# Turning values, keys and K with VectorE blocks and small transfers instead of TensorE transposes, in a hybrid retention/HGRN2 decoder layer

## The chip, the cores and the metric

The kernel runs on one core of one Trainium2 chip. The metric is device time in microseconds of one execution; lower is better. Before the change, three runs took 2565.3, 2567.76 and 2568.72 us.

## What is computed

One inference step of a decoder layer with model width 2048 for two groups of tokens that share the weights: a prompt of 256 tokens with 16 learned meta tokens ahead of it, and 8 single new tokens ("samples"), each with recurrent states of its own. All 280 tokens go through the dense products together. Per layer:

```
x <- LN1(alpha*x + 0.5*SwiGLU_1(x))
x <- LN2(alpha*x + Mixer(x))
x <- LN3(alpha*x + 0.5*SwiGLU_2(x))
```

The change lies in the mixer. One projection `x @ w_in` (2048 to 20480) gives ten parts. Retention has 8 heads of width 256, HGRN2 has 16 heads of width 128. In the reference a chunk of retention is:

```
inner = einsum('bhid,bhjd->bhij', q, k) * D
o = einsum('bhij,bhjv->bhiv', inner, v) + einsum('bhid,bhdv->bhiv', q_dec, S)
S_new = exp(lg * C) * S + einsum('bhjd,bhjv->bhdv', k_dec, v)
```

HGRN2 has the same form, with a decay for each key channel that depends on the data. The results are the tokens' outputs and the new states of both branches, for the prompt and for each sample.

Two of these products sum over tokens j: the state product (`k_dec` with `v`) and the output (`inner` with `v`). The matrix unit sums over partitions, so their operands must have tokens on the partitions, while the projection leaves channels on the partitions and tokens along the rows. Values and keys therefore have to be turned, 128x128 at a time.

## The kernel before

Every dense product is done in three matmuls per 128x128 weight block, in a reduced-precision fp32 format: each operand is split into a high and a low part, and high-high, low-high and high-low are summed (`dense`, line 204). Weights stream in units of eight blocks, 512 KB (`stream`, line 170): SP issues the DMA into one of three `raw` buffers, ScalarE casts the high part `whi` (line 188), VectorE subtracts for the low part `wlo` (line 189), each with three buffers, and TensorE's matmuls (line 218) follow.

The mixer runs over eight units `u`, one retention head and two HGRN2 heads each. For each, `project` runs the groups f, q_h, i_h, q_r, k_r, v_r and then the four gate groups of the unit before. A group has two output banks; one dense step is one k of its sixteen, six matmuls. After a group, `evacuate` (line 648) takes its two banks out of PSUM. The head's own small work is done by two Python generators, `mix_hg` (line 746) and `mix_ret` (line 1085), started after i_h and v_r. `pump` (line 617), called after each dense step, counts down each generator's wait; `yield n` means that it goes on n dense steps later. The order on TensorE is thus the order of the program, written by hand with these numbers. On the other engines and on SP's queue a scheduler orders by priority, with the weight stream ahead.

What the change touches, in this order within a unit:

- `evacuate` for i_h (lines 663 to 670) and v_r (682 to 686): ScalarE copies the two banks into the tile `v`, which both share (one buffer).
- `mix_hg`: GpSimd copies the first and last 16 tokens into `ends` (750, 751). TensorE transposes four 128x128 blocks of `v` (875) and the ends (878), ScalarE copies the result to `vth` (879). Later, `turned(h)` (976) transposes the decayed keys `K`, four blocks (982), ScalarE copies them to `kth` (983). Tiny GpSimd copies (769, 773) hold back the loads of the samples' states and values until a given point. The state product follows (1022 to 1030), and the samples' state updates (998, 999).
- `mix_ret`: GpSimd copies the last 24 tokens of k and v into `tails` (1103). For each half of the head TensorE transposes two blocks of v (1107) and two of k (1114), with the tails once (1116). ScalarE copies v to `vtr` (1108); `split` makes the high and low parts `vs` (1110); k is scaled by the decay and split into `ks` straight from PSUM (1129, 1130). Then come scores (1141), state product (1168), the samples' state update on ScalarE and VectorE (1192, 1198), its read on TensorE (1211), and outputs (1226). The samples' states, `ks` and `vs` share four buffers, `smr`.

Of the kernel before, what the change touches and what calls it, by code (L numbers as in the profile page):

```python
# [18 lines left out]
P = 128  # L19
# [109 lines left out]
def trunk(ctx: ExitStack, tc: tile.TileContext, A, O):  # L129
# [417 lines left out]
    with tc.tile_pool(name="yp", bufs=1) as yp:  # L547
# [7 lines left out]
        with tc.tile_pool(name="mp", bufs=1) as mp:  # L555
# [73 lines left out]
            def project(groups):  # L629
                for grp in groups:  # L630

                    bank = mx_bank if grp[0] == (QKV_ORDER[2], 0) else acc_bank
                    outs = [bank(f"pj_{n}{c}") for n, c in grp]
                    x0s = [NMETA if n in LIVE else 0 for n, _ in grp]
                    if grp[0] == (QKV_ORDER[0], 0):
                        outs = norm1.first(block, outs, x0s)
                    elif grp[0] == (QKV_ORDER[2], 0):
                        v = st["i_h"] = tmp("v", (P, 2, T))
                        outs = norm1.second(block, outs, x0s, (v[:, 0, :], v[:, 1, :]))
                    else:  # L640
                        dense(block, KC, outs, xh, xl, [slice(x0, T) for x0 in x0s], pump)
                        outs = [(o, None) for o in outs]
                    for j in range(0, len(grp), 2):
                        w = T - x0s[j]
                        (o0, b0), (o1, b1) = outs[j : j + 2]
                        evacuate(grp[j][0], grp[j][1], grp[j + 1][1], o0[:, :w], o1[:, :w], b0, b1)

            def evacuate(n, c0, c1, o0, o1, b0, b1):
# [14 lines left out]
                elif n == "i_h":  # L663
                    v = st.pop("i_h", None)
                    if v is None:
                        v = tmp("v", (P, 2, T))
                        nc.scalar.copy(v[:, 0, :], o0)
                        nc.scalar.copy(v[:, 1, :], o1)

                    start(mix_hg(c0 // 2, st["f"], st["k"], st["q"], v), {0: 20, 2: 46}.get(c0, 4))  # L670
                elif n in ("q_r", "k_r"):
                    sc, w, x0 = (1.0, TL, NMETA) if n == "q_r" else (KSC, T, 0)
                    r = tmp(n, (P, 2, w))
                    for j, (a, b, op) in enumerate(((cos, sin, ALU.subtract), (sin, cos, ALU.add))):
                        t = tmp("rot", (P, w), bufs=2)
                        for to, o, s, x in ((r[:, j, :], o0, b0, a), (t, o1, b1, b)):
                            nc.vector.scalar_tensor_tensor(
                                out=to, in0=o, scalar=sc if s is None else s, in1=x[:, x0:],
                                op0=ALU.mult if s is None else ALU.add, op1=ALU.mult)
                        nc.vector.tensor_tensor(out=r[:, j, :], in0=r[:, j, :], in1=t, op=op)  # L680
                    st[n] = r
                elif n == "v_r":
                    v = tmp("v", (P, 2, T))
                    nc.scalar.copy(v[:, 0, :], o0)
                    nc.scalar.copy(v[:, 1, :], o1)
                    start(mix_ret(c0 // 2, st["q_r"], st["k_r"], v), 24 if c0 == 2 else 3)
# [24 lines left out]

            NB2 = LP - 2 * P
# [33 lines left out]
            def mix_hg(u, f, k, q, v):  # L746

                calm = 2
                ends = tmp("ends", (P, 2, 2, NMETA))
                nc.gpsimd.tensor_copy(ends[:, :, 0, :], v[:, :, :NMETA])  # L750
                nc.gpsimd.tensor_copy(ends[:, :, 1, :], v[:, :, T - NMETA :])
# [13 lines left out]
                def load(h):  # L765

                    sms.append(tmp("smh", (P, NS, P), bufs=2))
                    vbs.append(tmp("vbh", (P, NS, P), bufs=2))
                    nc.gpsimd.tensor_copy(sms[h][:, 0, :1], kts[0][:, 0, :1] if h else acc[:, 15:16])
                    nc.sync.dma_start(sms[h], A["sg"][2 * u + h])  # L770

                def values(h):
                    nc.gpsimd.tensor_copy(vbs[h][:, 0, :1], kts[1][:, 0, :1] if h else acc[:, 2 * P + 15 : 2 * P + 16])
                    nc.sync.dma_start(vbs[h], vrow[h].partition_broadcast(P))
# [94 lines left out]
                vt = tmp("vth", (P, 2, 2, P))  # L869
                vrow = []  # L870
                for h in range(2):

                    pt = mx_bank("pt")
                    for b in range(2):
                        nc.tensor.transpose(pt[:, b * P : (b + 1) * P], v[:, h, NMETA + b * P : NMETA + (b + 1) * P], ident)
                    x = pt[:64, 2 * P : 3 * P]
                    if h:
                        nc.tensor.transpose(x, ends.rearrange("p c a t -> p (c a t)"), ident)
                    nc.scalar.copy(vt[:, h], pt[:, : 2 * P].rearrange("p (b f) -> p b f", b=2))
                    if h:  # L880
# [93 lines left out]
                kts = []  # L974

                def turned(h):
                    kt = tmp("kth", (P, 2, P), bufs=2)
                    kts.append(kt)
                    pt = mx_bank("ptk")
                    for b in range(2):  # L980
                        t0 = NMETA + b * P
                        nc.tensor.transpose(pt[:, b * P : (b + 1) * P], K[:, h, t0 : t0 + P], ident)
                    nc.scalar.copy(kt, pt[:, : 2 * P].rearrange("p (b f) -> p b f", b=2))
# [20 lines left out]
                turned(0)  # L1004
                load(1)
                yield 4
                turned(1)
# [5 lines left out]
                if u != 1:  # L1013
                    samples(1)
                    yield 4 if u == 0 else 5

                Ss = []
                for h in range(2):
# [4 lines left out]
                    for b in range(2):  # L1023
                        nc.tensor.matmul(pst[:, (b + 1) * P : (b + 2) * P], kts[h][:, b, :], vt[:, h, b, :], start=True, stop=True)
# [9 lines left out]
                yield (8, 11, 45)[min(u, 2)]  # L1034
# [11 lines left out]
                def outputs(h):  # L1046
                    po = mx_bank("po")
                    for b in range(2):
                        o = po[:, b * P : (b + 1) * P]
                        nc.tensor.matmul(o, vt[:, h, b, :], acc[:, (2 * h + b) * P : (2 * h + b + 1) * P], start=True, stop=False)  # L1050
# [26 lines left out]
            def centre(x):  # L1077

                np_, n = x.shape[0], x.shape[1]
                m = tmp("cen", (P, n))[:np_]  # L1080
                nc.vector.tensor_reduce(out=m, in_=x, op=ALU.add, axis=mybir.AxisListType.X)
                nc.vector.tensor_scalar(out=m, in0=m, scalar1=1.0 / 256, scalar2=None, op0=ALU.mult)
                nc.vector.tensor_tensor(out=x, in0=x, in1=m.unsqueeze(2).to_broadcast([np_, n, 256]), op=ALU.subtract)

            def mix_ret(u, q, k, v):
                vt = tmp("vtr", (P, 2, 2, P))

                ks, vs = (tmp(n, (P, 2, 2, 2 * P), dt=F32R, bufs=4, tag="smr") for n in ("ks", "vs"))
# [13 lines left out]
                for i, x in enumerate((k, v)):  # L1102
                    nc.gpsimd.tensor_copy(tails[:, 2 * i : 2 * i + 2, :NB], x[:, :, 2 * P :])
                for c in range(2):
                    pt = mx_bank("pt")
                    for b in range(2):
                        nc.tensor.transpose(pt[:, b * P : (b + 1) * P], v[:, c, b * P : (b + 1) * P], ident)
                    nc.scalar.copy(vt[:, :, c, :], pt[:, : 2 * P].rearrange("p (b f) -> p b f", b=2))
                    f = slice(c * P, (c + 1) * P)
                    split(vs[:, 0, :, f], vs[:, 1, :, f], vt[:, :, c, :])  # L1110
                    yield 1
                    pt = mx_bank("pt")
                    for b in range(2):
                        nc.tensor.transpose(pt[:, b * P : (b + 1) * P], k[:, c, b * P : (b + 1) * P], ident)
                    if c == 0:
                        nc.tensor.transpose(pt[:, 2 * P : 3 * P], tails.rearrange("p i t -> p (i t)"), ident)
# [5 lines left out]
                    todo = [(pt[:, b * P : (b + 1) * P], dec[:, b, u : u + 1], [ks[:, 0, b, f]], 0, ks[:, 1, b, f]) for b in range(2)]  # L1122
# [11 lines left out]
                vts = [vt[:, 0], vt[:, 1], vs2]  # L1134
# [25 lines left out]
                yield 4  # L1160

                for c in range(2):
                    pst = mx_bank("psr")
                    f = slice(c * P, (c + 1) * P)
                    todo = [(ks[:, i, b, f], vs[:, j, b, :].rearrange("p (c f) -> p c f", c=2)) for b in range(2) for i, j in ((0, 0), (0, 1), (1, 0))]
# [13 lines left out]
                centre(vt.rearrange("p b c f -> p b (c f)"))  # L1179
# [24 lines left out]
                yield (11 if u == 0 else 15) + 2 * calm  # L1204
# [18 lines left out]
                for c in range(2):  # L1223
                    po = mx_bank("por")
                    for b, (col, l0, n, nk) in enumerate(SCORES):
                        nc.tensor.matmul(po[:, l0 : l0 + n], vts[b][:, c, :], scrs[b], start=b == 0, stop=b == 2)
# [150 lines left out]
```

## Time and profile before

| | |
|---|---|
| runs | 2565.3, 2567.76, 2568.72 us; median 2567.76 |
| profiled execution | span 2563.9 us, first to last instruction (its time outside the span isn't given) |
| TensorE clock granted | 1.000 |
| dense matmuls: ffn 1, the mixer's projections, w_out, ffn 2 | 5.3 to 745, 745.0 to 1760.5, 1760.7 to 1848.8, 1848.9 to 2547.6 us |
| DMA | 536.26 MB, mean 209 GB/s; 62.0% of the 16 engines' span on SP's queue |

The profile is one execution as the hardware profiler saw it. Its page gives busy time by engine, the span in slices, the chain of work that ended last, and the costliest groups of instructions; the trace behind it can be asked for a timeline, for waits, for DMA issues, and for busy time in chosen stretches. A group's row has the program line, engine, operation, tiles and shapes, count, busy time and mean ns of one, and behind the second bar the idle time before it with what ended that. Matmuls overlap, so a matmul's duration is longer than its share of TensorE's pace.

### The profile page before, as it was taken

Reading aid. Unit: us, or ns where it says so; the run is one execution under the profiler, and the core shown is the slowest. Engines: PE = TensorE matmul, PEld = TensorE weight load, DVE = VectorE, ACT = ScalarE, POOL = GpSimd, SP = SyncE. Lnnn points to the kernel's source line nnn. Section 1 sums busy time; section 2 is a strip of 40 time slices with the busy share of each in tenths; the row PEclk is TensorE's granted clock in tenths of the full one; section 3 lists DMA queues with packets and bytes.
Section 4 is the critical chain, followed back from the end, with each engine's and each line's share of the span. In section 5 each row is a group of like instructions: output and inputs, shape, how many; then the busy total and the mean of one; then the engine's idle time right before and its main releaser. Section 6 shows DMA issues by size and latency. Waiting matters only on the chain.

```text
span 2563.9 us, 56275 instructions
## 1 busy us (share of the span) xinstructions
PE 2553.4 (100%) x23424; PEld 2534.4 (99%) x23424; DVE 1702.8 (66%) x2827; ACT 1392.2 (54%) x2186; POOL 57.0 (2%) x152
## 2 busy tenths in 40 slices
PE   9999999999999999999999999999999999999999
PEld 9999999999999999999999999999999999999998
DVE  6444544475569878777777777777885555556555
ACT  5444444444456767767676666675564444444443
POOL 0000000000000000000000000000000000000000
PEclk9999999999999999999999999999999999999999
DMA  7555555555555876767676767675556565565554
GB/s 244 183 187 183 187 182 184 186 182 186 184 201 180 287 265 232 264 214 260 212 264 215 259 223 255 224 239 188 196 190 197 194 197 195 194 196 195 195 195 149
DMA packets 156897, 536.26 MB, mean 209 GB/s; under 512 B 17952, under 2 KB 25952, under 8 KB 156640
## 3 DMA queue, kind: packets, MB, share of 16 engines
q1 hardware_dynamic: 156352, 532.37, 62.0%
q8 instruction: 183, 3.00, 0.5%
q14 instruction: 74, 0.61, 0.1%
q10 hardware_dynamic: 288, 0.29, 0.0%
HBM read 501.99 MB, written 30.61 MB: 208 GB/s over the span
## 4 chain that ended last, share of the span: by engine, by line
PE 96%; DVE 2%; ACT 0%; issue 0%; DMA 0%; SPq 0%; ACTq 0%; DVEq 0%
PE up L218 36%; PE dn L218 19%; PE pj_i_h L218 3%; PE pj_g_r L218 3%; PE pj_q_h L218 3%; PE pj_g_h L218 3%; PE pj_a_r L218 3%; PE pj_a_h L218 3%; PE pj_f L218 3%; PE pj_q_r L218 3%; PE pj_k_r L218 3%; PE wo L218 3%; PE pj_v_r L218 3%; DVE wlo L189 1%; PE pqr L1211 1%; PE psr L1168 0%
## 5 line engine op out<-in xcount | busy, mean ns | idle before, releaser
L189 DVE TENSOR_TENSOR wlo<-raw,whi 128x1024 fp32r<-128x1024 f32 (+1 forms) x869 | 1062.2, 1223 | 740.7 <-ACT whi L188 737.3
L188 ACT CAST whi<-raw 128x1024 fp32r<-128x1024 f32 (+1 forms) x870 | 905.7, 1042 | 909.2 <-PE up L218 411.0
L218 PE MATMUL up<-xh,whi 128*128 128x280 f32 (+1 forms) x2624 | 725.6, 280 | 0.6 <-ACT whi L188 0.6
L218 PE MATMUL up<-xh,wlo 128*128 128x280 f32 (+1 forms) x2624 | 725.8, 280 | 0.4 <-DVE wlo L189 0.3
L218 PE MATMUL up<-xl,whi 128*128 128x280 f32 (+1 forms) x2624 | 725.4, 279 | 0.0
L218 PEld LDWEIGHTS up<-xh,wlo 128*128 128x128 f32 x2624 | 492.6, 189 | 1.0 <-DVE wlo L189 1.0
L218 PEld LDWEIGHTS up<-xh,whi 128*128 128x128 f32 x2624 | 492.6, 189 | 0.8 <-ACT whi L188 0.8
L218 PEld LDWEIGHTS up<-xl,whi 128*128 128x128 f32 x2624 | 492.6, 189 | 0.0
L218 PE MATMUL dn<-hh,whi 128*128 128x280 f32 (+1 forms) x1376 | 384.7, 280 | 0.0
L218 PE MATMUL dn<-hh,wlo 128*128 128x280 f32 (+1 forms) x1376 | 384.3, 279 | 0.0
L218 PE MATMUL dn<-hl,whi 128*128 128x280 f32 (+1 forms) x1376 | 384.3, 279 | 0.0
L218 PEld LDWEIGHTS dn<-hh,whi 128*128 128x128 f32 x1376 | 260.1, 189 | 0.1
L218 PEld LDWEIGHTS dn<-hl,whi 128*128 128x128 f32 x1376 | 260.1, 189 | 0.1
L218 PEld LDWEIGHTS dn<-hh,wlo 128*128 128x128 f32 x1376 | 260.1, 189 | 0.0
L218 PE MATMUL pj_k_r<-xh,whi 128*128 128x280 f32 x256 | 74.2, 290 | 0.0
L218 PE MATMUL pj_g_r<-xh,whi 128*128 128x264 f32 x256 | 74.0, 289 | 0.0
L218 PE MATMUL pj_v_r<-xh,whi 128*128 128x280 f32 x256 | 73.8, 288 | 0.0
L218 PE MATMUL pj_v_r<-xh,wlo 128*128 128x280 f32 x256 | 72.4, 283 | 0.3 <-DVE wlo L189 0.3
L218 PE MATMUL pj_g_h<-xh,whi 128*128 128x264 f32 x256 | 72.7, 284 | 0.0
L218 PE MATMUL pj_k_r<-xh,wlo 128*128 128x280 f32 x256 | 72.4, 283 | 0.0
L218 PE MATMUL pj_v_r<-xl,whi 128*128 128x280 f32 x256 | 72.3, 283 | 0.0
L218 PE MATMUL pj_k_r<-xl,whi 128*128 128x280 f32 x256 | 72.3, 283 | 0.0
(421 smaller groups left out, 5263.4 us busy)
## 6 DMA issues: line engine op xcount, KB each, us to landing
raw<-in_w_up SPq DMA_DIRECT2D x343, 512.0 KB, 4.1
raw<-in_w_in SPq DMA_DIRECT2D x320, 512.0 KB, 4.3
raw<-in_w_dn SPq DMA_DIRECT2D x172, 512.0 KB, 3.5
smr<-in_sr SPq DMA_DIRECT2D x32, 512.0 KB, 5.0
out_srs<-smr SPq DMA_DIRECT2D x32, 512.0 KB, 6.7
raw<-in_w_out SPq DMA_DIRECT2D x32, 512.0 KB, 3.9
vbr<-vrd SPq DMA_DIRECT2D x32, 256.0 KB, 4.1
smh<-in_sg SPq DMA_DIRECT2D x16, 512.0 KB, 5.2
```

What stands on the lines that cost most here:

```text
L188: nc.scalar.copy(hi[:, j:jn, :], raw[:, j:jn, :])
L189: nc.vector.tensor_tensor(out=lo[:, j0:j1, :], in0=raw[:, j0:j1, :], in1=hi[:, j0:j1, :].bitcast(F32), op=ALU.subtract)
L218: nc.tensor.matmul(o, w, t, start=start, stop=stop)
L1211: nc.tensor.matmul(pq[32 * j : 32 * j + 32, :256], qdr_at[c][:, 32 * b : 32 * b + 32], sms[2 * e + c][:, j, :], start=e + c == 0, stop=e + ...
```

## The change

All sixteen 128x128 transposes per unit on TensorE that serve v of both branches, k and K are replaced. VectorE's `transpose` turns each 32x32 block in place within its 32 partitions and 32 columns. A new function, `turned_over`, then moves the blocks to where they belong in a full transpose: 16 transfers from SBUF to SBUF, each of 32 partitions in rows of 32 values, issued on SP's queue by a generator of its own, one per dense step (`rate` 1) or two (`rate` 2).

- Values are turned at evacuation, by VectorE straight from PSUM into `v`; ScalarE copies only the ends, or the tails, and GpSimd's copies of those go. The very first i_h group goes through two spare tiles.
- k is turned right after its rotary passes, into the same single buffer `v`, and moved into the low half of `ks`, which is allocated there. The decay and split then work in place in SBUF.
- K is turned into the memory of `k` and moved into that of `f`; the tile `kth` goes.
- The split of the values and the retention state product come 6 dense steps later, the samples' update with them, and the wait ahead of the samples' read is 6 shorter. From unit 2 on, the HGRN2 state product comes 8 later and the wait behind it is 8 shorter.
- The transposes of ends, tails and the meta tokens stay on TensorE.

```diff
                 elif n == "i_h":
-                    v = st.pop("i_h", None)
-                    if v is None:
-                        v = tmp("v", (P, 2, T))
-                        nc.scalar.copy(v[:, 0, :], o0)
-                        nc.scalar.copy(v[:, 1, :], o1)
-
-                    start(mix_hg(c0 // 2, st["f"], st["k"], st["q"], v), {0: 20, 2: 46}.get(c0, 4))
+                    ends = tmp("ends", (P, 2, 2, NMETA))
+                    vt = tmp("vth", TURNED)
+                    v = tmp("v", TURNED)
+                    for j, o in enumerate(st.pop("i_h", (o0, o1))):
+                        nc.vector.transpose(v[:, j].rearrange("p b t -> p (b t)"), o[:, NMETA:LP])
+                        nc.scalar.copy(ends[:, j, 0, :], o[:, :NMETA])
+                        nc.scalar.copy(ends[:, j, 1, :], o[:, T - NMETA : T])
+                    turned_over(vt, v)
+                    start(mix_hg(c0 // 2, st["f"], st["k"], st["q"], ends, vt), {0: 20, 2: 46}.get(c0, 4))
...
+                    if n == "k_r":
+                        st["ks"] = ks = tmp("ks", (P, 2, *TURNED[1:]), dt=F32R, bufs=4, tag="smr")
+                        z = tmp("v", TURNED)
+                        nc.vector.transpose(z.rearrange("p c b t -> p c (b t)"), r[:, :, : 2 * P])
+                        turned_over(ks[:, 1].bitcast(F32), z, 2)
                     st[n] = r
                 elif n == "v_r":
-                    v = tmp("v", (P, 2, T))
-                    nc.scalar.copy(v[:, 0, :], o0)
-                    nc.scalar.copy(v[:, 1, :], o1)
-                    start(mix_ret(c0 // 2, st["q_r"], st["k_r"], v), 24 if c0 == 2 else 3)
+                    vt = tmp("vtr", TURNED)
+                    v = tmp("v", TURNED)
+                    for j, o in enumerate((o0, o1)):
+                        nc.vector.transpose(v[:, j].rearrange("p b t -> p (b t)"), o[:, : 2 * P])
+                        nc.scalar.copy(tails[:, 2 + j, : T - 2 * P], o[:, 2 * P :])
+                    turned_over(vt, v, 2)
+                    start(mix_ret(c0 // 2, st["q_r"], st["k_r"], st["ks"], vt), 24 if c0 == 2 else 3)
...
+            TURNED = (P, 2, 2, P)
...
+            def turned_over(out, z, rate=1):
+
+                def transfers():
+                    for i in range(4):
+                        for j in range(4):
+                            nc.sync.dma_start(
+                                out[32 * j : 32 * j + 32, :, :, 32 * i : 32 * i + 32],
+                                z[32 * i : 32 * i + 32, :, :, 32 * j : 32 * j + 32])
+                            if (4 * i + j + 1) % rate == 0:
+                                yield 1
+
+                start(transfers(), 1)
...
-                def turned(h):
-                    kt = tmp("kth", (P, 2, P), bufs=2)
-                    kts.append(kt)
-                    pt = mx_bank("ptk")
-                    for b in range(2):
-                        t0 = NMETA + b * P
-                        nc.tensor.transpose(pt[:, b * P : (b + 1) * P], K[:, h, t0 : t0 + P], ident)
-                    nc.scalar.copy(kt, pt[:, : 2 * P].rearrange("p (b f) -> p b f", b=2))
+                kt = f.rearrange("p h t -> p (h t)")[:, : 4 * P].rearrange("p (h b t) -> p h b t", h=2, b=2)
+
+                def turned():
+                    z = k.rearrange("p h t -> p (h t)")[:, : 4 * P].rearrange("p (h b t) -> p h b t", h=2, b=2)
+                    nc.vector.transpose(z.rearrange("p h b t -> p h (b t)"), K[:, :, NMETA:])
+                    turned_over(kt, z, 1 if steady else 2)
...
-                    yield 4 if u == 0 else 5
+                    yield 4 if u == 0 else 13
...
-                yield (8, 11, 45)[min(u, 2)]
+                yield (8, 11, 37)[min(u, 2)]
...
-                    todo = [(pt[:, b * P : (b + 1) * P], dec[:, b, u : u + 1], [ks[:, 0, b, f]], 0, ks[:, 1, b, f]) for b in range(2)]
+                    todo = [(ks[:, 1, c, b].bitcast(F32), dec[:, b, u : u + 1], [ks[:, 0, c, b]], 0, ks[:, 1, c, b]) for b in range(2)]
...
-                yield 4
+                yield 8
+                for c in range(2):
+                    split(*(vs[:, i, :, c * P : (c + 1) * P] for i in range(2)), vt[:, c])
+                    yield 1
+                yield 2
...
-                yield (11 if u == 0 else 15) + 2 * calm
+                yield (5 if u == 0 else 9) + 2 * calm
```

In `mix_ret` the old transposes of v and k and their `yield 1` per half are gone with the code that filled `vs` there, which is why the state product is 6 and not 8 steps later.

More of the change, by code (lines that the diff above doesn't have):

```diff
@@ L637, in project @@
                     elif grp[0] == (QKV_ORDER[2], 0):
-                        v = st["i_h"] = tmp("v", (P, 2, T))
-                        outs = norm1.second(block, outs, x0s, (v[:, 0, :], v[:, 1, :]))
+                        first = st["i_h"] = [tmp("rot") for _ in range(2)]
+                        outs = norm1.second(block, outs, x0s, first)
                     else:
@@ L1002, in samples @@
                     nc.sync.dma_start(O["sgs"][2 * u + h], sm)
-                turned(0)
+                turned()
                 load(1)
                 yield 4
-                turned(1)
                 values(1)
@@ L1101, in mix_ret @@
                 nc.sync.dma_start(dt, A["dtab"][u])
-                for i, x in enumerate((k, v)):
-                    nc.gpsimd.tensor_copy(tails[:, 2 * i : 2 * i + 2, :NB], x[:, :, 2 * P :])
+                nc.gpsimd.tensor_copy(tails[:, :2, :NB], k[:, :, 2 * P :])
                 for c in range(2):
[L1105 to L1114, printed above, removed]
                     if c == 0:
+                        pt = mx_bank("pt")
                         nc.tensor.transpose(pt[:, 2 * P : 3 * P], tails.rearrange("p i t -> p (i t)"), ident)
```

42 lines of the change are left out of this document (16 added, 26 removed), and 2 rows, old and new, of the table rows.

## The prediction

> **What bounds the kernel now.** I read the first page first: span, busy time and the chain.
>
> ```profile
> span 2563.9 us, 56275 instructions
> PE 2553.4 (100%) x23424; PEld 2534.4 (99%) x23424; DVE 1702.8 (66%) x2827; ACT 1392.2 (54%) x2186; POOL 57.0 (2%) x152
> PE 96%; DVE 2%; ACT 0%; issue 0%; DMA 0%; SPq 0%; ACTq 0%; DVEq 0%
> ```
>
> TensorE is busy nearly throughout, and 96% of the chain is its work. So an instruction taken off TensorE is worth what it takes of TensorE's pace, unless something else then comes late. Next I cut the mixer, where the whole change lies, into stretches. The columns are PE, PEld, DVE, ACT and POOL busy, granted clock, DMA share, GB/s.
>
> ```profile
> 790.00:820.00 30.00, 28.07 (x229) 27.12 (x228) 28.68 (x63) 15.45 (x30) 4.25 (x4) 1.00 0.49 163
> 820.00:990.00 170.00, 169.82 (x1819) 165.85 (x1820) 143.13 (x319) 123.98 (x253) 12.01 (x25) 1.00 0.75 261
> 990.00:1720.00 730.00, 730.00 (x7405) 719.78 (x7404) 572.92 (x1135) 492.93 (x924) 38.16 (x92) 1.00 0.71 240
> ```
>
> From 990 to 1720 us, roughly six of the eight heads, TensorE sits idle for nothing, with VectorE at 573 of 730 and the DMA engines at 0.71. From 790 to 820, head 0, it is different: VectorE is busy 28.68 of 30 and TensorE loses 1.93. The view of waits for TensorE in that place says on what:
>
> ```profile
> PE pt L1116 <- POOL tails L1103: 0.9, 1, 0.9
> PE pj_f L218 <- DVE wlo L189: 0.7, 1, 0.7
> PE pj_v_r L218 <- DVE wlo L189: 0.3, 1, 0.3
> ```
>
> **What leaves TensorE.** The groups of the four kinds of transpose that go:
>
> ```profile
> L1107 PE MATMUL pt<-ident,v 128*128 128x128 f32 x32 | 6.2, 276 | 0.0
> L982 PE MATMUL ptk<-ident,K 128*128 128x128 f32 x32 | 6.1, 273 | 0.0
> L1114 PE MATMUL pt<-ident,k_r 128*128 128x128 f32 x32 | 6.1, 273 | 0.0
> L875 PE MATMUL pt<-ident,v 128*128 128x128 f32 x32 | 6.1, 273 | 0.0
> ```
>
> That is 128 transposes, 24.5 us of busy time; but matmuls overlap, so the mean of 273 ns is not what one costs. The timeline around a pair shows the cost:
>
> ```profile
> 1266.32 0.28 PE L218 MATMUL pj_k_r<-xl,whi 128*128 128x280 f32 x1
> 1266.43 0.28 PE L218 MATMUL pj_k_r<-xh,wlo 128*128 128x280 f32 x1
> 1266.56 0.38 PE L982 MATMUL ptk<-ident,K 128*128 128x128 f32 x2
> 1266.69 0.37 PE L218 MATMUL pj_k_r<-xh,whi 128*128 128x280 f32 x1
> 1266.89 0.28 PE L218 MATMUL pj_k_r<-xl,whi 128*128 128x280 f32 x1
> ```
>
> Dense matmuls start 0.12 us apart (1266.32, 1266.43). From the one before the pair to the second one after it is 1266.89 - 1266.43 = 0.46 us where two steps of 0.12 would be 0.24. So two transposes cost 0.22 us, one 0.11, and 128 of them **14.1 us**. The transposes of the ends and tails stay. The Trainium skill (VectorE: DVE Perf Modes, The three transpose paths) lists a 128x128 bf16 transpose on TensorE at 390 ns, and in its rules for kernel authors it advises TensorE for a 128x128 transpose when PSUM is a fit destination, which speaks against this change; by its figure the sum would be 128 x 0.390 = 49.9 us, an estimate from that page, and the trace's pace does not agree.
>
> One stall goes as well: the 0.9 us at 820 us, where the tails' transpose waited for a GpSimd copy that itself waited for ScalarE's copy of the values. After the change ScalarE writes the values' tails directly. I take -0.9, bounds 0 to -0.9, since the weights are late in the same place.
>
> **What VectorE and ScalarE get.** Per head: two transposes of 256 columns from PSUM for the HGRN values, two for the retention values, one of 512 for k and one of 512 for K. The trace has no VectorE transpose; the nearest rows by size are these (the first reads PSUM), with the ScalarE copies that go, and a narrow one for those that come:
>
> ```profile
> L830 DVE TENSOR_TENSOR acch<-pl,ident 128x256 f32<-128x256 f32 x16 | 6.2, 422 | 0.2
> L1083 DVE TENSOR_TENSOR vtr<-vtr,cen 128x512 f32<-128x512 f32 x8 | 5.5, 692 | 0.3
> L983 ACT COPY kth<-ptk 128x256 f32<-128x256 f32 x16 | 6.0, 373 | 8.2 <-PE ptk L982 8.1
> L684 ACT COPY v<-pj_v_r 128x280 f32<-128x280 f32 x8 | 3.1, 392 | 1.6 <-PE pj_v_r L218 1.6
> L863 ACT COPY acch<-pl 16x64 f32<-16x64 f32 (+1 forms) x48 | 10.6, 221 | 4.2 <-DVE acch L836 3.5
> ```
>
> VectorE gains 4 x 0.42 + 2 x 0.69 = 3.1 us a head, 18 in the six heads of the long stretch, where it is idle for 157 of 730. ScalarE loses some ten copies of 0.37 to 0.39, 3.8 us, and gains six narrow ones of 0.2, 1.3 us. On average this is hidden. Where the cover is gone it is paid: in head 0 between 790 and 820, VectorE's spare is 1.3 us and TensorE already waits for its weight splits. There come the two value transposes of i_h, that of k and the two of v_r: 0.84 + 0.69 + 0.84 = 2.4 us. I take **+2.4**, bounds 0 and +2.4.
>
> **The tight place in every head.** A dense group reads a weight pair only once VectorE's wlo is done. Mostly wlo is early; about 31 us after the retention values are projected it is not. In order of time, with the read of the sample states and the sum of the stretch from 1284 to 1320 behind:
>
> ```profile
> 1283.95 0.28 PE L218 MATMUL pj_g_r<-xh,whi 128*128 128x264 f32 x1
> 1285.31 1.22 DVE L189 TENSOR_TENSOR wlo<-raw,whi 128x1024 fp32r<-128x1024 f32 x1
> ...
> 1312.10 1.27 DVE L1198 SCALAR_TENSOR_TENSOR smr<-vbr,sro,smr 128x256 f32<-128x256 f32 x3
> 1313.63 1.22 DVE L189 TENSOR_TENSOR wlo<-raw,whi 128x1024 fp32r<-128x1024 f32 x1
> 1314.86 0.28 PE L218 MATMUL pj_g_r<-xh,whi 128*128 128x264 f32 x1
> L1211 PE MATMUL pqr<-smr,qdr x32: 379/379/403, 1317.9 to 1319.5; 128*32 128x256 f32 x32
> sum 36.00, PE 36.00 PEld 34.86 DVE 29.96 ACT 23.91 POOL 2.53; mean PE 6.00 PEld 5.81 DVE 4.99 ACT 3.99 POOL 0.42
> ```
>
> The wlo of 1285.31 is the third of the four that the group begun at 1283.95 reads; two before it take 48 matmuls at 0.11, 5.3 us, so it is wanted from 1289.2 and was ready at 1286.53: 2.7 us early. The later one ends at 1314.85 and its pair is used from 1314.86: no slack. And the change moves the state product and the sample update six dense steps later while the read at L1211 stays: six steps of six matmuls at 0.11 us are 4.0 us, so the last update, ended at 1313.37, comes at 1317.4, before 1317.9 and well before the second half of that read. The order of ScalarE, VectorE and SP work after the state product is the old one, only later, nearer to the 3 us of small matmuls that let the weights catch up. What is new before it is 0.84 us of VectorE for v_r, with 1.5 us of ScalarE copies gone. Unknown cost: between nothing (TensorE doesn't wait there now, so nothing is to be gained) and 0.84 + 1.0 us (half the second read) a head, 14.7 us in eight. I take **+3**, nearest to nothing because VectorE has 6.0 of the 36 us free.
>
> **The transfers.** Each turn adds 16 transfers of 32 partitions in rows of 128 B, 16 KB; four turns in eight heads are 512 transfers on SP's queue, which also issues the weights. The price of an issue and of small packets, and of ScalarE's pass over a weight load and a rotary pass on VectorE:
>
> ```profile
> L188 ACT CAST whi<-raw 128x1024 fp32r<-128x1024 f32 (+1 forms) x870 | 905.7, 1042 | 909.2 <-PE up L218 411.0
> L677 DVE SCALAR_TENSOR_TENSOR k_r<-pj_k_r,cos 128x280 f32<-128x280 f32 x8 | 3.6, 448 | 3.6 <-PE pj_k_r L218 3.6
> 1284.26 0.34 SPq L1002 DMA_DIRECT2D out_sgs<-smh  x1
> 1285.16 1.44 SPq L1030 DMA_DIRECT2D out_sgp<-Sh  x2
> 1289.44 0.33 SPq L185 DMA_DIRECT2D raw<-in_w_in  x1
> raw<-in_w_in SPq DMA_DIRECT2D x230, 512.0 KB, 4.4
> out_srp<-sro SPq DMA_DIRECT2D x12, 128.0 KB, 2.3
> out_sgp<-Sh SPq DMA_DIRECT2D x12, 64.0 KB, 5.0
> DMA packets 319, 0.19 MB, mean 161 GB/s; under 512 B 48, under 2 KB 304, under 8 KB 319
> q1 hardware_dynamic: 319, 0.19, 52.0%
> ```
>
> The last two rows are one stretch of 1.2 us (970.95 to 972.15), nearly all packets of 512 B and less: 0.52 x 16 x 1.2 us / 319 = 31 ns each, an upper bound for rows of 128 B. A transfer has 128 of them and a few for its semaphore, about 0.28 us of all 16 engines, 512 of them 143 us in some 930: from 0.71 to at most 0.86. Bandwidth is not the limit on average.
>
> Issue is nearer to it. An issue takes 0.34 us, 0.72 where SP was held. A weight load of eight blocks lasts 24 matmuls, 2.9 us. At one transfer a dense step SP needs 4 x 0.34 + 0.33 = 1.7 us of that; at two (k, v, and K in heads 0 and 1) 8 x 0.34 + 0.33 = 3.1, or 6.1 at 0.72. A burst of 16 at two a step is thus late by 0.4 us at the low price and 6.4 at the high one. The cover: of the three raw buffers' 8.7 us, a load, ScalarE's and VectorE's pass take 4.4 + 1.04 + 1.22, leaving 2.0, and outside the tight place wlo is some 2.7 early: about 5. I take the low price, as 0.33 to 0.34 is what a queue that isn't held takes, and cost it at nothing. The single buffer of the turned values is used by k and then by v 11.5 us later: six rotary passes of 0.45 and the turn (3.4), the burst (5.8) and a landing (2.3) are 11.5, just in time; landing as late as 5.0, VectorE would wait 2.7 us with the weight splits behind it, which is all of wlo's lead there.
>
> **Sum.** -14.1 - 0.9 + 2.4 + 3 = **-9.6 us**: span 2554.3. The trace gives the profiled run's span only; the median of the runs shown, 2567.76, stands 3.9 us above it, work outside the span that I leave alone. Predicted 2558.
>
> **The rivals.** *The tight place eats the gain* (no change). All transposes leave before the tight place, 16 x 0.11 = 1.8 us a head; if wlo there is paced by SP, DMA and VectorE alone, TensorE only arrives earlier and waits. In six heads that is 10.6 us: -14.1 - 0.9 + 2.4 + 10.6 = -2.0, 2566. For it: the zero slack. Against: that work follows the state product, which TensorE itself issues, after the removed transposes.
>
> *SP's queue becomes the bound* (slower). If a transfer costs SP over 0.63 us (16 x 0.63 + 0.66 against 5.7 is the 5 us of cover), weights come late in each of the 18 bursts; at 0.72 by 6.4 - 5 = 1.4 us, 25 in all: 2558 + 25 = 2583. For it: the 1.44 us for two and DMA shares near 1 around the states' loads. Against: most rows at 0.33. The Trainium skill (DMA: Bandwidth & Descriptors, Rules for kernel authors) says that under 64 KB a transfer is mostly overhead, which stands on this rival's side; no run here shows it for moves within SBUF.
>
> *More than forecast*: both VectorE terms nothing, -15.0: 2553. The transposes certainly go, so that the change does nothing is no rival of its own.
>
> **How the numbers follow.** A measurement of this kernel tells about 0.2%, 5 us, from no change. Forecast with the rival above it 0.66 (2550 to 2562), tight place 0.17, SP 0.17. Low end: 2553 less the runs' 2.5 us of spread; high end 2575, where SP costs 17 of its 25 us. Faster 0.66, same 0.17, slower 0.17.
>
> **What would show it.** Right: 128 fewer matmuls, no groups at the four lines, dense matmuls still 0.12 apart, a head about 1.5 us shorter, TensorE idle below 5 us between 820 and 1720. Wrong: TensorE waiting for wlo or whi right after the bursts, with SP issues over 0.6 us (SP); waits of 1 to 2 us before the sample read of each head (tight place); VectorE transposes much over 0.7 us.

## The result, and the profile after

The changed kernel takes 2792.74 us, median of four runs (2790.28 to 2796.48), against 2567.28 of the kernel before: ratio 1.0881, 95% interval 1.0865 to 1.0896. It is 225 us slower where 10 us less were forecast. Two single runs of later kernels, 3725.94 us at a granted clock of 0.67 (one move a turn) and 5186.65 us at 0.90 (the HGRN2 values alone), were slow ones and are left out of the times below. The profiled execution is the run of 2790.28 us. From its page come the span, the busy time, the DMA share of SP's queue, the chain of waits and one group; the last line is SP's issues for one of the four turns (least, median and longest ns):

```profile
span 2788.5 us, 56771 instructions
PE 2581.3 (93%) x23296; PEld 2555.6 (92%) x23296; DVE 1725.7 (62%) x2875; ACT 1375.1 (49%) x2156; POOL 35.0 (1%) x128
q1 hardware_dynamic: 230080, 540.79, 60.4%
PE 82%; SPq 5%; DVE 5%; DMA 5%; ACT 2%; issue 1%; POOL 0%; DVEq 0%; ACTq 0%; POOLq 0%
L1116 PE MATMUL pt<-ident,tails 128*128 128x128 f32 x8 | 3.6, 447 | 128.8 <-ACT tails L694 128.8
L743 SPq DMA_DIRECT2D ks<-v x128: 585/599/1168, 819.8 to 1874.7; - x128
```

The 128 transposes are gone (23,424 matmuls before). TensorE now stands idle for 207 us of the span (2788.5 - 2581.3; 10.5 before), and the chain has SP's queue, VectorE and DMA in it. As a share of the span, which is longer, the DMA engines are no busier (62.0% before). The waits of TensorE, then those on the new transfers (total, times, longest):

```profile
PE pt L1116 <- ACT tails L694: 128.8, 8, 17.8
PE psr L1172 <- ACT vs L225: 40.5, 6, 8.1
PE pst L1034 <- DMA f<-k: 12.4, 1, 12.4
PE pj_k_r L218 <- DVE q_r L679: 5.2, 1, 5.2
...
ACT ks L1129 <- DMA ks<-v: 100.8, 7, 15.1
DVE v L693 <- DMA ks<-v: 91.9, 7, 13.8
ACT vs L225 <- DMA vtr<-v: 42.9, 7, 8.1
```

How one such wait comes about, in the unit of 1550 us (timeline of the changed kernel: start, duration, engine, line, operation; in brackets the idle time before it):

```profile
1553.07 0.48 SPq L185 DMA_DIRECT2D raw<-in_w_in  x1
1553.60 0.59 SPq L743 DMA_DIRECT2D ks<-v  x1
1554.22 0.60 SPq L743 DMA_DIRECT2D f<-k  x1
1554.87 0.60 SPq L743 DMA_DIRECT2D ks<-v  x1
1555.57 0.53 SPq L185 DMA_DIRECT2D raw<-in_w_in  x1
...
1565.81 1.24 SPq L743 DMA_DIRECT2D ks<-v  x2
1568.37 0.78 DVE L693 STREAM_TRANSPOSE v<-pj_v_r 128x256 f32<-128x256 f32 x2 [13.41 <-DMA ks<-v]
1568.37 0.69 ACT L1129 ACTIVATE ks<-ks,dec 128x128 fp32r<-128x128 f32 x2 [14.76 <-DMA ks<-v]
1569.08 0.18 ACT L694 COPY tails<-pj_v_r 128x24 f32<-128x24 f32 x1
1569.78 0.45 PE L1116 MATMUL pt<-ident,tails 128*128 128x128 f32 x1 [16.32 <-ACT tails L694]
1569.88 0.57 PE L218 MATMUL pj_g_r<-xh,whi 128*128 128x264 f32 x1
1570.24 0.43 PE L218 MATMUL pj_g_r<-xl,whi 128*128 128x264 f32 x1
```

SP issues without a pause, 0.60 us a transfer. K's 16 (`f<-k`) and k's 16 (`ks<-v`) stand between each other and the weights between both, so k's tile is whole only at 1568. Two steps wait for that: ScalarE's scaling of k (14.8 us), and VectorE's turn of the retention values (13.4 us), which writes the one buffer `v` that k's moves still read. The tails' copies come after both, and behind them the next weight cast; TensorE, whose order is fixed, waits 16.3 us for the tails. Then v's 16 transfers begin, and the state product waits up to 8.1 us for them.

The start of the same dense matmul, in the kernel before and the changed one:

| | before | changed | later by |
|---|---|---|---|
| a gate group, behind unit 2's state product | 1070.62 | 1159.30 | 88.7 |
| last one ahead of the HGRN2 state product in the kernel before | 1154.95 | 1242.76 | 87.8 |
| unit 3's retention values projected | 1157.62 | 1244.31 | 86.7 |
| tails' wait passed | 1172.33 | 1276.40 | 104.1 |
| state product passed | 1183.13 | 1298.89 | 115.8 |

Down to the second row unit 3 gains 0.9 us. The eight transposes of the HGRN2 values and of K stood there, so this is 0.11 us each. The next 1.1 us is no gain: it is the HGRN2 state product, which the change moves behind the retention values. Then the unit loses 17.4 and 11.7 us, although the other eight transposes leave there, and small products that were moved are in both numbers. In all it is 27 us a unit. The delay is already 62 us when unit 2 has projected its retention values; units 0 and 1 bring that. So the transposes' gain is there, and the losses are some fifteen times as large.

### The profile page after: what moved, and what is told of

It reads as the page before. It is cut to its first block, busy times and chain, and to the rows that moved or that the text cites. A ratio compares the mean times of both kernels' runs of the same rounds, so it can differ in the third digit from the quotient of the medians.

```text
span 2788.5 us, 56771 instructions
## 1 busy us (share of the span) xinstructions
PE 2581.3 (93%) x23296; PEld 2555.6 (92%) x23296; DVE 1725.7 (62%) x2875; ACT 1375.1 (49%) x2156; POOL 35.0 (1%) x128
## 4 chain that ended last, share of the span: by engine, by line
PE 82%; SPq 5%; DVE 5%; DMA 5%; ACT 2%; issue 1%; POOL 0%; DVEq 0%; ACTq 0%; POOLq 0%
PE up L218 32%; PE dn L218 17%; SPq L743 4%; PE pj_i_h L218 3%; PE wo L218 3%; PE pj_q_r L218 3%; PE pj_q_h L218 3%; PE pj_f L218 3%; PE pj_k_r L218 3%; PE pj_g_h L218 3%; PE pj_a_h L218 3%; PE pj_g_r L218 2%; PE pj_a_r L218 2%; DVE wlo L189 2%; PE pj_v_r L218 1%
## 5 line engine op out<-in xcount | busy, mean ns | idle before, releaser
L1116 PE MATMUL pt<-ident,tails 128*128 128x128 f32 x8 | 3.6, 447 | 128.8 <-ACT tails L694 128.8
```

## The experiments

Theory: SP's in-order queue, at 0.60 us an issue, makes turned tiles late, and what stands behind their consumers. Rivals: the single buffer `v`; the moves themselves (bytes, pieces) in the DMA engines; the later products; VectorE's turns.

**What an issue costs.** Idle transfers behind the mixer's last group of the kernel before, such as

```diff
             project(gate_groups(HR - 1))
+            for rnd in range(2):
...
+                for j in range(4):
+                    for i in range(2):
+                        nc.sync.dma_start(vt[32 * j : 32 * j + 32, :, :, 32 * i : 32 * i + 32], q4(z)[32 * i : 32 * i + 32, :, :, 32 * j : 32 * j + 32])
```

> The kernel before, with some 48 idle transfers of several shapes within SBUF at the end of the mixer, which nobody reads; it measures what SP takes to issue each. If the price goes by the pieces: 32 partitions of 4 pieces of 128 B 0.60 us, 32 partitions of one piece of 512 B and 128 partitions of one piece about 0.33, 128 partitions of 4 pieces of 128 B over 1 us. If it goes by the shape alone (more dimensions, a slower issue): both shapes with 4 pieces about 0.60, both with one about 0.33. If moves within SBUF are dear as such: all about 0.60.

The medians of the five shapes were 0.59 to 0.64 us: neither pieces nor partitions matter to this price. One more run of that kind set loads (`A["cos"]` to a tile) beside moves.

> The kernel before with idle DMAs behind the mixer's last group, twice: 16 loads from HBM of 32 partitions by 512 B, 4 of 128 partitions by 512 B, and 16 moves within SBUF of 32 partitions by 512 B, back to back. If the 0.60 us belongs to moves within SBUF, the loads are issued in 0.33 to 0.35 and the moves in 0.60. If it belongs to a queue kept full, the loads after the first few take 0.60 too.

Its issues (`vth`, `vtr` are loaded from HBM, `f<-K` is within SBUF; least, median and longest ns):

```profile
L1253 SPq DMA_DIRECT2D vth<-in_cos x32: 311/420/1061, 1718.9 to 1746.8; - x32
L1256 SPq DMA_DIRECT2D vtr<-in_cos x8: 334/430/526, 1712.5 to 1748.4; - x8
L1263 SPq DMA_DIRECT2D f<-K x32: 507/564/1195, 1652.6 to 1748.9; - x32
```

Taken singly, in a row a load mostly took 0.42 us (0.31 to 0.33 after a pause) and a move 0.59 to 0.60 (0.51 after a pause). Both ideas were half right: in this run a move within SBUF took some 0.18 us longer than a load, and an issue in a row some 0.09 longer than one after a pause.

**One move, four, eight.** Each turn's sixteen transfers become one, or four of 128 partitions, or eight of 64. These kernels leave out the exchange of the blocks, so their turned tiles are not transposes and their results are not the layer's. The edit for one move:

```diff
-                    for i in range(4):
-                        for j in range(4):
-                            nc.sync.dma_start(
-                                out[32 * j : 32 * j + 32, :, :, 32 * i : 32 * i + 32],
-                                z[32 * i : 32 * i + 32, :, :, 32 * j : 32 * j + 32])
...
+                    nc.sync.dma_start(out, z)
```

> The changed kernel, but each turn's sixteen transfers are replaced by one that moves the whole tile without exchanging its blocks (the exchange of blocks is left out). Queue theory (SP's issue time of the transfers is what everything waits for): 64 transfers a head become 4, the waits of about 17 us before the tails' transpose and 8 us before the state product go, and what is left of the change is TensorE's gain of 14 us less a few us on VectorE: 2550 to 2560 us. Rival (turning on VectorE and the later state product cost time by themselves): well above 2567 us even so.

> The same kernel as the one-move run (changed kernel with one move of a whole tile in place of each turn's sixteen; the exchange of the blocks is left out), taken again for a profile. Time 2592 to 2602 us as before. Its profile should name the other 32 us: if VectorE's turns and the tails that stand behind them, waits of the tails' transpose remain (2 to 3 us a head); if the later products, waits before psr, pst and pqr; if the moves left over (one a turn, 0.6 us) nothing is late on SP.

> The same with four moves a turn, each of 128 partitions in rows of 128 B, four times the bytes. By the queue's issue time k's and K's together take 5 us, which is about the cover: 2598 to 2615 us, no further than the one-move kernel's 2599 but for a little. If pieces of 128 B were the cost, far above that, since there are as many of them as in the changed kernel.

> The changed kernel with eight moves a turn in place of sixteen, each of 64 partitions and twice the bytes (the same bytes in all; the blocks are not exchanged, so the turned tiles are not the transposes). An issue of 0.60 us whatever its shape gives a turn of 5 us on SP, and k's and K's together 10 in place of 20. If the queue's issue time is the cost, k's tile lands some 8 us after the retention values' group and not 16: 2630 to 2670 us. If bytes or pieces were the cost, no less than 2770.

| moves a turn | SP for k's and K's turn | tails' wait in all | TensorE idle in all | median | ratio |
|---|---|---|---|---|---|
| 1 | 1.3 us | 16.1 us | 40.5 us | 2598.05, again 2598.57 | 1.0112, again 1.0123 [1.0108, 1.0138] |
| 4 | 5.2 | 14.8 | 54.5 | 2616.99 | 1.0192 [1.0177, 1.0207] |
| 8 | 10.3 | 52.2 | 92.8 | 2667.99 | 1.0397 [1.0381, 1.0412] |
| 16 (the change) | 20.6 | 128.8 | 207.2 | 2792.74 | 1.0881 [1.0865, 1.0896] |

(The second column is an estimate, moves by 0.645 us, an issue and the gap behind it. Idle is the span less TensorE's busy time; the trace columns of the first row are from its second run.) Four moves missed the expected band by 2 us and one move by 38; eight fell in it. The bytes are the same in all four, and four, eight and sixteen also have the same pieces of 128 B. So the 176 us from four moves to sixteen are the number of issues. The 18 from one to four may be issues or pieces, as one move has rows of 2 KB. About 5 us of burst are nearly covered; beyond that the tails' wait grows by 37 us for 5.1 us more a unit, then by 77 for 10.3. The one-move kernel kept 32 us that the theory had not foretold; they come below.

**Other queues.** The same transfers on GpSimd's queue, and, with `nc.scalar` in the same place, on ScalarE's.

```diff
-                            nc.sync.dma_start(
+                            nc.gpsimd.dma_start(
```

> The changed kernel with all 512 transfers issued on GpSimd's queue; the work is the same. If SP's time per issue was the cost, weight loads no longer stand behind transfers, and two queues work beside each other: if GpSimd issues one in 0.6 us too, a burst of 16 still takes 10 us, k's and K's one after the other 20, so the late blocks remain and only the late weights go: 2640 to 2740 us. If GpSimd issues faster than SP, below 2640. If the moves are slow in the DMA engines and not on the queue, no change: 2780 to 2800.

> The changed kernel with all 512 transfers issued on ScalarE's queue; the work is the same. If an issue takes its 0.6 us on whatever engine issues it, ScalarE gains 300 us of work in the mixer, in front of weight casts, and TensorE waits for whi instead: 2750 to 2900 us. If the 0.6 us was SP's alone and ScalarE hands a transfer over in 0.1 us or less: below 2640.

GpSimd: 2700.67 us, 1.0519 [1.0503, 1.0535]; ScalarE: 2783.72, 1.0845 [1.0829, 1.0861]. An issue takes about as long there:

```profile
L743 POOL DMA_DIRECT2D ks<-v x128 | 69.4, 549 | 23.7 <-DMA ks<-v 8.4 <-issue 5.8 <-DVE v L686 5.7
```

The bursts now have no weights and no loads of the states between them: from unit 2 on k's sixteen take 9.6 to 12.3 us from first to last issue (18.5 to 20.1 on SP) and v's 8.6 to 9.1 (17.0 to 19.1), with K's ahead of k's. With that 92 us come back, the tails' wait halves (62.5 us) and the state product's wait for v is gone. On ScalarE's queue an issue takes 0.59 us as well and stands among the weight casts and the tails' copies themselves, for which TensorE waits 98.5 us; for `whi`, which was expected, it waits only 8.0.

**The single buffer, and K left out.**

```diff
-                        z = tmp("v", TURNED)
+                        z = tmp("vbr", (P, 2, 256), bufs=2).rearrange("p c (b t) -> p c b t", b=2)
```

and, in the other run, the old `turned(h)` on TensorE in place of the new one.

> The changed kernel, but the turned k has a buffer of its own and no longer shares one with the turned values. Single-buffer theory: VectorE's 92 us of waiting for k's transfers before it turns v go, and with them most of the 129 us that TensorE waits for the tails: 2670 to 2720 us. Queue theory: the decay and split of k wait for the same transfers on ScalarE and VectorE, in front of the tails' copies and the weights, so that at most 3 us a head are gained: 2765 to 2795 us.

> The changed kernel, but K is turned by TensorE as before: 48 instead of 64 transfers a head, and none of K's between those of k. Queue theory: k's sixteen transfers end some 10 us earlier in each head, the wait for the tails falls from about 17 to 5 to 8 us, K's transposes cost 3.5 us again: 2690 to 2730 us. Single-buffer theory: k's transfers have the queue as before for themselves, no more than 3 us a head: 2765 to 2795 us.

A buffer apart: 2792.46, 1.0877 [1.0861, 1.0893], no change in time, but TensorE's waits moved. With one step in the unit of 1550 us:

```profile
PE pst L1034 <- DMA f<-k: 69.2, 5, 14.9
PE psr L1172 <- ACT vs L225: 60.7, 8, 15.8
PE pst L1034 <- DMA vtr<-v: 29.5, 2, 15.1
PE pt L1116 <- ACT tails L694: 16.1, 7, 3.3
...
1554.00 0.18 ACT L694 COPY tails<-pj_v_r 128x24 f32<-128x24 f32 x1 [0.73 <-DVE v L693]
1569.11 1.28 ACT L1129 ACTIVATE ks<-ks,dec 128x128 fp32r<-128x128 f32 x4 [9.56 <-DMA ks<-vbr]
```

The tails' copies now come right behind VectorE's turn and 15 us ahead of k's scaling, and most of the tails' wait goes, as the single-buffer theory had said. But the next products in TensorE's order need the same late tiles, and the four rows sum to 175.5 us; in the changed kernel the tails, `psr` and `pst` sum to 181.7. So the shared buffer decides where TensorE waits, and SP's queue how long. K back on TensorE, 384 transfers left: 2739.41, 1.067 [1.0655, 1.0686], 53 us gained; the theory's band was missed by 9. With k's and v's bursts left, TensorE still waits 80.5 us for the tails and 40.3 before the state product.

**The 32 us of the one-move kernel.** First the later products alone, in the kernel before (part of the edit).

```diff
-                    yield 4 if u == 0 else 5
+                    yield 4 if u == 0 else 13
...
-                yield 4
+                yield 10
```

(and the waits behind them shorter by as much).

> The kernel before with one part of the change alone: both state products, and what hangs on them, come six to eight dense steps later; all turns stay on TensorE. The one-move run left some 32 us over the kernel before that the 512 issues don't explain. If the later products cost them (the sample reads stay where they were, so the updates that feed them have less room): 2590 to 2605 us, and TensorE waits in the profile before the reads pqr and pq. If they cost nothing: within 5 us of 2567, and the 32 us lie with VectorE's turns or the chain of waits on them.

2573.07 us, 1.0025 [1.0015, 1.0035]: some 6 us, between the two expectations. In the one-move kernel's own profile the tails' wait was the largest row, so it was moved away:

```diff
+                yield 4
                 for c in range(2):
                     if c == 0:
                         pt = mx_bank("pt")
...
-                yield 8
+                yield 4
```

> The one-move kernel (block exchange left out) with the retention mixer's start, its tails' transpose first, four dense steps later, and the state product where it was. In the one-move profile TensorE waits 2.3 us a head there, 16.1 in all, for ScalarE's copies of the tails, which stand behind four scalings of k and a weight cast. If that order makes the wait: it goes, 2580 to 2586 us. If the wait moves on to the next small matmuls: 2595 to 2602.

2599.28: the wait went (no row of it is left) and came back elsewhere, in part as waits for `wlo`, `cen` and `q`. Next, much of the loss lay in unit 1. ScalarE's first step of unit 1, on f, in the kernel before, and in the changed one:

```profile
833.30 0.40 ACT L653 ACTIVATE f<-pj_f 128x280 f32<-128x280 f32 x1
```

```profile
907.57 0.70 ACT L653 ACTIVATE f<-pj_f 128x280 f32<-128x280 f32 x2 [0.80 <-PE pst L1034]
```

It starts 74 us later, right behind unit 0's state product: the turned K lies in f's memory, which that product frees. Until then f's group keeps its two of the four PSUM banks that the groups share (`ps_a`, four buffers). With two left, i_h, q_r and k_r of unit 1 each wait for the group ahead to be taken out. The store was undone in the one-move kernel (`kth` tiles again), and done alone in the kernel before, where TensorE still turns K:

```diff
-                    kt = tmp("kth", (P, 2, P), bufs=2)
+                    kt = f.rearrange("p h t -> p (h t)")[:, 2 * P * h : 2 * P * h + 2 * P].rearrange("p (b t) -> p b t", b=2)
```

> The one-move kernel (block exchange left out) with the turned K in two tiles of its own, where the kernel before kept it, and not in f's memory; one move a head more. If the store in f's memory holds head 1's dense groups: 2580 to 2586 us, head 1's sigmoid of f directly behind its group, and no wait of i_h, q_r or k_r there. If VectorE's turns do it: 2596 to 2602 as before.

> The kernel before with one thing of the change alone: ScalarE writes the turned K, which TensorE still turns, into f's memory. No VectorE turn, no transfer, nothing later. If the store holds head 1: 2578 to 2588 us and the waits of i_h, q_r and k_r in head 1 appear in this profile. If not: within 3 us of 2567.

Undone: 2579.27, 1.0047 [1.0033, 1.0061], 19 us less, and f's step is back at 832 us (first line below). Alone: 2581.93, 1.0059 [1.0046, 1.0073], 15 us more, with the late step and the waits in its profile:

```profile
832.46 0.40 ACT L653 ACTIVATE f<-pj_f 128x280 f32<-128x280 f32 x1 [0.53 <-PE pj_f L218]
...
891.62 0.70 ACT L653 ACTIVATE f<-pj_f 128x280 f32<-128x280 f32 x2 [0.80 <-PE pst L1024]
PE pj_k_r L218 <- DVE q_r L677: 5.2, 1, 5.2
PE pj_i_h L218 <- DVE q L240: 3.9, 2, 2.6
```

Of the other 12 us, about 6 may be the later products. The rest, and what eats the 14 us of transposes in the one-move kernel, stay open: the waits move with the order on ScalarE and VectorE, and no run settles them one by one.

**Is anything left to gain?** HGRN2 values and K turned by VectorE with their moves on GpSimd's queue, retention as before; then the same freed of what its profile showed; then the HGRN2 values alone. Parts of the edits to the kernel before:

```diff
+                            nc.gpsimd.dma_start(
...
-                        nc.gpsimd.tensor_copy(meta[:, :, NMETA + NS * i : NMETA + NS * (i + 1)], fk[:, i])
+                        nc.vector.tensor_copy(meta[:, :, NMETA + NS * i : NMETA + NS * (i + 1)], fk[:, i])
```

(the second edit in the second run alone, with K's turn in two `kth` tiles).

> The kernel before with half of the change: HGRN values and K turned by VectorE, the retention values and k by TensorE as before, and the 256 transfers on GpSimd's queue, which is idle. 64 transposes fewer are 7 us of TensorE. The values are wanted 20 us and more after their burst, K's tile some 21 us after its own (10 us at 0.6 us an issue), so neither burst should be late, and SP carries what it did: 2560 to 2565 us, below both kernels. If the moves themselves or VectorE's turns cost TensorE elsewhere, or the later state product does (6 us for both products by its own run): 2567 to 2580.

> The run of the HGRN half on GpSimd's queue with its two hindrances taken away: the turned K in tiles of its own (32 transfers of half the size for it, two a step), and the copies of the gates that ScalarE and VectorE waited for (33 us in that profile) on VectorE instead of GpSimd. From 2622: less 15 for the store in f, less 20 to 30 for the gates: 2568 to 2590. Below 2563 would need the 7 us of the transposes whole; I expect the later state product to take them back.

> The kernel before with the HGRN values alone turned by VectorE, their 16 transfers a head on GpSimd's queue, K in its own tiles, products where they were. 32 transposes fewer are 3.5 us; the values are wanted some 20 us after their burst. 2562 to 2566 us if VectorE's turns and the moves lie beside other work; 2567 to 2575 if GpSimd's small copies, which feed ScalarE and the loads, come late behind 16 issues of 0.55 us.

2622.1 us, 1.0213 [1.0198, 1.0229]; 2641.36, 1.0286 [1.0272, 1.03]; 2567.5, 1.0002 [0.9993, 1.0011]. The first two missed. GpSimd was busy 2% of the time before, but its small copies feed others. In the first run ScalarE waited for the gates' copies, with weight casts behind; in the second those were on VectorE, K took twice the issues, and TensorE waited for GpSimd's copy of the tails. These are the largest waits that came; no run shows that they are the whole loss:

```profile
ACT smh L1001 <- POOL meta L993: 33.2, 6, 6.5
PE pj_g_r L218 <- ACT whi L188: 13.4, 6, 3.9
```

```profile
PE pt L1129 <- POOL tails L1116: 30.9, 6, 7.8
```

The values alone gain 0.4 us a unit in the last units, as 4 x 0.11 foretells, and lose about 4 once in units 0 and 1. No version beat the kernel before.

## Why the prediction was wrong

*The transposes, -14.1.* Right: the eight that leave before the state product give 0.9 us a unit, 0.11 each, as forecast.

*VectorE, +2.4.* The durations were right, bounded from rows of other operations (0.42 and 0.69); what they cost TensorE in head 0 no run shows by itself:

```profile
L693 DVE STREAM_TRANSPOSE v<-pj_v_r 128x256 f32<-128x256 f32 x16 | 6.2, 428 | 99.3 <-DMA ks<-v 91.9 <-DMA smr<-in_sr 7.3
L686 DVE STREAM_TRANSPOSE v<-k_r 128x512 f32<-128x512 f32 x8 | 5.7, 712 | 2.9 <-DMA vth<-v 2.7
```

*The tails' wait, -0.9.* Wrong, and by sign: it became the largest row. The change moves the copy from GpSimd to ScalarE, and the prediction did not ask what would stand in front of it there: VectorE's turn of the values, which waits for the buffer that k's moves read, and k's scaling, which until then had read PSUM and now waits for a DMA. With a buffer apart 16.1 us of it are left.

*The tight place, +3 (0 to 14.7).* The later products alone cost 6, within the bounds.

*The transfers, at nothing.* This is the step that failed, in three places. The price was 0.34 us, read from a store and a weight load that stood alone; moves in a row take 0.60. The count in flight was 16; from unit 2 on it is 32, because K's turn at one a step runs into k's at two. And the lateness was weighed against the weights' cover alone, while the tiles' own consumers have none: the tails, k's scaling and the products stand where TensorE's order has them, and k's burst takes 20 us.

The third is the largest. With 0.645 us an issue the prediction's own rule gives a burst late by 16 x 0.645 + 0.66 - 5.7 = 5.3 us against a cover of 5, some 5 us in 18 bursts. With K on TensorE, so that 16 are in flight, TensorE still waits 80.5 us for the tails. The cover of about 5 us agrees with the small cost of four moves a turn (5.2 us for both bursts, 18 us over one move), but it was worked out for the weights and not for the consumers, so the agreement may be luck. That bandwidth is no limit fits: four moves have the pieces and bytes of sixteen and cost 176 us less.

*The rival of SP's queue* had the place and the side, at 0.72 us and +25 us, but not the mechanism. It had the weights come late, with waits for `wlo` or `whi` as its sign; in the changed kernel TensorE waits under 2 us for them and 182 for turned tiles and tails. Its break-even of 0.63 us was worked out for the weights, so it says nothing of the consumers, and 0.60 was already far too much for those.

*The single buffer*, priced at up to 2.7 us a head, made VectorE wait up to 13.8, and TensorE behind it for the tails; taking it away moved those waits and saved nothing.

*Where the turned K is kept* was not priced at all: 15 to 19 us. The diff showed it, one line after the `kth` tile goes.

## What to carry to other kernels

Price a DMA issue from a row where the queue is full and the transfer is of the same kind, count all bursts that are in flight together on an in-order queue, and compare their length with the time until the consumer, not with an average load. When a wait is taken away and the time stays, look where the wait went. When a tile's memory is reused, ask who gets it next and what that one holds while it waits. An engine at 2% busy is not free if others wait for its small copies.

## What the runs showed of the hardware

After a long wait TensorE runs at half its pace. In the changed kernel, whose TensorE stood from 1553.5 to 1569.8 us (columns: stretch and its length, PE, PEld, DVE, ACT, POOL busy, granted clock, DMA share, GB/s):

```profile
1552.00:1556.60 4.60, 1.45 (x13) 1.25 (x12) 2.97 (x5) 1.61 (x4) 0.00 (x0) 1.00 0.67 195
1556.60:1569.00 12.40, 0.00 (x0) 0.00 (x0) 0.63 (x2) 0.63 (x2) 0.00 (x0) 0.50 0.44 134
1570.00:1573.70 3.70, 3.70 (x18) 3.70 (x18) 1.43 (x3) 2.98 (x7) 0.00 (x0) 0.50 0.63 163
1573.70:1578.00 4.30, 4.30 (x36) 4.20 (x35) 3.09 (x8) 1.38 (x5) 0.00 (x0) 1.00 0.57 206
```

The granted clock falls to 0.50 some 3.1 us after TensorE stopped and is back 3.9 us after it went on. In those 3.7 us 18 matmuls start, where 36 do in the next 4.3, so about 2 us are lost on top of the wait. Over the whole kernel this adds up: TensorE is busy 28 us longer than before (2581.3 against 2553.4) although 14 us of transposes are gone. So an estimated 42 of the loss is busy time and not waiting, and sixteen waits of over 3 us at some 2 us each would make 32 of it. The Trainium skill (TensorE: Matmul & The Clock Gate, Part 1) says that the array drops to half its clock after about 3.4 us of idleness and needs as much activity to return; this trace agrees, with 3.1 and 3.9 us.

The Trainium skill (DMA: Bandwidth & Descriptors, Anatomy of one DMA) puts the sequencer's dispatch of a DMA from GpSimd at some 50 ns and its descriptors at a small, variable cost, with most of the fixed cost in completion. Here GpSimd spent 549 ns on each 16 KB move, so the measurement decides: in this kernel, where sixteen are issued in a row, the time of the issues is what counts.
